# Turning attention probabilities with 16-bit DMA transposes instead of TensorE

## The chip, the cores and the metric

The kernel runs on one core of a Trainium2 chip. Its measure is the device time of one execution in microseconds. The five engines of a core are TensorE (PE in the rows, with PEld for its weight loads), VectorE (DVE), ScalarE (ACT), GpSimd (POOL) and SyncE (SP), whose queue issues most DMAs. Each engine runs its own list of instructions in order and waits on semaphores for the others. The DMA engines, 16 of them, move data beside all that.

## The reference, cut to what matters

A trunk of four layers works on 256 tokens of width 2048, in float32. Each layer normalises its input, multiplies it by one wide weight, splits the product into mixer inputs, memory queries and gates, runs a mixer (layers 0 and 3: a spatial gate; layer 1: forgetting attention; layer 2: differential attention) and a cross-attention to 256 memory tokens, gates both, and multiplies by an output weight. The part that the change touches is the second half of every attention, here that of the memory:

```python
logits = jnp.einsum('bshd,bmhd->bhsm', q, mem_k).astype(jnp.float32) * (HEAD_DIM ** -0.5)
p = jax.nn.softmax(logits, axis=-1).astype(mem_v.dtype)
return jnp.einsum('bhsm,bmhd->bshd', p, mem_v).reshape(B, S, MEM_WIDTH)
```

The probabilities `p` come out with the query along the partitions. TensorE needs the key there to multiply by the values, so every 128x128 block of `p` has to be turned. Differential attention turns the difference of two softmaxes.

The memory tokens are normalised too, `mem_n = rms_norm(mem, mem_norm_g)`. The kernel multiplies the raw memory by the weights and applies each token's factor afterwards.

## The kernel before

**Slots.** All weights, about 310 MB, stream through once. They are cut into 592 pieces of 128x1024 float32, and the program is a sequence of 592 *slots*, one for each piece. In a slot TensorE runs 12 matmuls of 128x512 (`slot_product`, lines 186 to 188): the weight and the activations are each split into a high and a low part, and three of the four products are taken. Eight slots make a *product* of 512 columns.

**What stands in one slot.** `between_slots` writes the rest of a slot in this order: `tick()` advances every running task (a Python generator) by one step; `split_until` splits the weight piece four slots ahead into its parts (ScalarE's cast at line 119, VectorE's subtraction at line 120); `load_until` issues the load of the piece eight slots ahead on SP (line 106); `run_late` writes what the tasks put off. There are four buffers for raw pieces and four for split ones. Engine lists are in the order written, so what a task writes in a slot stands ahead of that slot's cast, subtraction, load and matmuls.

**Attention.** `attention_task` (line 587) handles eight *units*, a unit being one head of one block of 128 queries. Step n writes, in order: the finishing of unit n-1 (a reciprocal; for differential attention the difference of the two softmaxes), the product of unit n-3 with the values (`av`, line 606), the turning of unit n-2 (`nc.tensor.transpose`, line 615, into a PSUM tile, and ScalarE's copy `pt` of it at line 619), the scores of unit n (lines 514, 531, 556), and the eviction of unit n-3's result by VectorE (line 629, or 627). A step takes one slot, for differential attention two for the first eight. There are 10 attentions: one of the memory in each layer and three in each of layers 1 and 2. A unit of the memory has two blocks to turn; in the other attentions the first four units have one and the last four two.

**The DMA transpose already in the kernel.** Other tensors are turned by `turn` and `join` (lines 360 to 375): ScalarE copies a 128x512 float32 tile, seen as 16-bit halves, into a plane of high halves and one of low halves (line 362); one `dma_start_transpose` on SP turns both planes (line 367); VectorE puts the halves together again (line 372).

**The start.** The first 16 slots make two products in turn, from the memory. The result of the first is scaled by the memory tokens' factors `r_mem` into `mvv` (ScalarE, line 404). `token_rms` computes these: over some slots it loads the memory's rows in four steps of two 256 KB tiles (SP, line 310), squares and sums them on ScalarE (line 303), and puts off the finish (VectorE lines 294 and 290, then a power on GpSimd, line 291). It is spawned with `delayed(3, ...)`, so that its first step falls into the third slot on.

**The end of layer 2.** The last differential attention ends near the end of the last gate product. `gate_task` multiplies its result with the gate (line 662), turns it with `turn` and `join`, and splits it into the parts `bh` and `bl` (lines 678 and 684) that the output product reads; these parts are needed in that product's seventh and eighth slots.

Of the kernel before, what the change touches and what calls it, by code (L numbers as in the profile page):

```python
# [9 lines left out]
F32 = mybir.dt.float32  # L10
F32R = mybir.dt.float32r
U16 = mybir.dt.uint16
# [8 lines left out]
P = 128  # L21
# [22 lines left out]
def trunk_kernel(  # L44
# [372 lines left out]
        yield from gen  # L417

    spawn(load_transposed(mem_t, "b", 4 * KT, bparts, early, 1, 2))
    spawn(delayed(3, token_rms(mem, r_mem)))  # L420
    first_accs = pair_product(lambda kp: bparts[kp])
    for i in range(DEPTH):
        acc = first_accs[0] if i == 0 else chunk_product(lambda kp: bparts[kp])
# [88 lines left out]
    def mem_scores(qt, mk, h, t):  # L512
        s = ps_s.tile([P, CW], F32, tag="s", name="s")
        nc.tensor.matmul(  # L514
            s[:, :S], qt[:, h, t * P : (t + 1) * P], mk[:, h * S : (h + 1) * S],
            start=True, stop=True,
        )
        st = small.tile([P, 8], F32, tag="sc", name="st")
        nc.vector.tensor_reduce(st[:, 0:1], s[:, :S], AX.X, ALU.max, negate=True)  # L519
        p = tmp.tile([P, S], F32, tag="p", name="p", bufs=4)  # L520
        late.append(
            lambda: nc.scalar.activation(
                p, s[:, :S], AF.Exp, bias=st[:, 0:1], accum_out=st[:, 1:2]
            )
        )
        return p, st, lambda: nc.vector.reciprocal(st[:, 2:3], st[:, 1:2])

    def fox_scores(qt, kt, h, hh, t, bias, cq):
# [10 lines left out]
        )  # L539
        st = small.tile([P, 8], F32, tag="sc", name="st")  # L540
        nc.vector.tensor_reduce(st[:, 0:1], lg[:, :w], AX.X, ALU.max, negate=True)
        p = tmp.tile([P, S], F32, tag="p", name="p", bufs=4)
        late.append(
            lambda: nc.scalar.activation(
                p[:, :w], lg[:, :w], AF.Exp, bias=st[:, 0:1], accum_out=st[:, 1:2]
# [4 lines left out]
    def diff_scores(qt, kt, h, t, bias):  # L550
# [10 lines left out]
        for m in range(2):  # L561
# [3 lines left out]
                scalar=BIG, op0=ALU.add, op1=ALU.min, accum_out=st[:, m : m + 1],  # L565
            )
            lgs.append(lg)
        ps = [tmp.tile([P, S], F32, tag="p", name="p", bufs=4) for m in range(2)]

        def exps():  # L570
            for m in range(2):
# [16 lines left out]
    def attention_task(scores, vv, finish, ready, diff=False, tiles=lambda t: t + 1):  # L588
# [2 lines left out]
        units = [(t, h) for t in range(2) for h in range(4)]  # L591
        mo = [tmp.tile([P, CW], F32, tag="mo", name="mo", bufs=6) for t in range(2)]
        made, turned = {}, {}
        for n in range(len(units) + 3):
            if 0 <= n - 1 < len(units):
                made[n - 1][2]()
            tb = None
            if 0 <= n - 3 < len(units) or 0 <= n - 2 < len(units):
                tb = ps_t.tile([P, CW], F32, tag="t", name="tb")
            if 0 <= n - 3 < len(units):  # L600
                t, h = units[n - 3]
                pt, done_st = turned.pop(n - 3)
                f = slice(h * HD, (h + 1) * HD)
                av = tb[:, 2 * P : 2 * P + HD]
                for j in range(tiles(t)):
                    nc.tensor.matmul(  # L606
                        av, pt[:, j * P : (j + 1) * P], vv[:, j, f],
                        start=(j == 0), stop=(j == tiles(t) - 1),
                    )
            if 0 <= n - 2 < len(units):  # L610
                t, h = units[n - 2]
                p, st, _ = made.pop(n - 2)
                nk = tiles(t)
                for j in range(nk):
                    nc.tensor.transpose(  # L615
                        tb[:, j * P : (j + 1) * P], p[:, j * P : (j + 1) * P], ident
                    )
                pt = tmp.tile([P, S], F32, tag="pt", name="pt")
                nc.scalar.copy(pt[:, : nk * P], tb[:, : nk * P])  # L619
                turned[n - 2] = (pt, st)  # L620
            if n < len(units):
                made[n] = scores(*units[n])
            if 0 <= n - 3 < len(units):
                t, h = units[n - 3]
                f = slice(h * HD, (h + 1) * HD)
                if diff:
                    nc.vector.tensor_copy(mo[t][:, f], av)
                else:
                    nc.vector.tensor_scalar(mo[t][:, f], av, done_st[:, 2:3], None, ALU.mult)
# [474 lines left out]
```

## Time and profile before

| | |
|---|---|
| median of 3 runs | 1737.36 us (1737.34 to 1737.95) |
| the profiled execution | 1737.19 us |
| its span, first to last instruction | 1735.4 us |
| TensorE busy | 1726.9 us |
| VectorE busy | 1076.3 us |
| ScalarE busy | 985.9 us |
| DMA queue of SP and ACT, share of 16 engines | 69.5% |

The span is what lies between the first and the last instruction; 1.8 us of the execution's time lie around it. The clock granted to TensorE was 1.000 of full speed as the mean of the whole span. Matmuls are pipelined: an instruction's own duration in the profile is longer than the distance to the next one's start, and the ends are modelled. The distance of starts is what an instruction takes from the stream.

### The profile page before, as it was taken

Reading aid. Unit: us, or ns where it says so; the run is one execution under the profiler, and the core shown is the slowest. Engines: PE = TensorE matmul, PEld = TensorE weight load, DVE = VectorE, ACT = ScalarE, POOL = GpSimd, SP = SyncE. Lnnn points to the kernel's source line nnn. Section 1 sums busy time; section 2 is a strip of 40 time slices with the busy share of each in tenths; the row PEclk is TensorE's granted clock in tenths of the full one; section 3 lists DMA queues with packets and bytes.
Section 4 is the critical chain, followed back from the end, with each engine's and each line's share of the span. In section 5 each row is a group of like instructions: output and inputs, shape, how many; then the busy total and the mean of one; then the engine's idle time right before and its main releaser. Section 6 shows DMA issues by size and latency. Waiting matters only on the chain.

```text
span 1735.4 us, 21890 instructions
## 1 busy us (share of the span) xinstructions
PE 1726.9 (100%) x7918; PEld 1423.2 (82%) x7918; DVE 1076.3 (62%) x1539; ACT 985.9 (57%) x1349; POOL 129.0 (7%) x156
## 2 busy tenths in 40 slices
PE   9999999999999999999999999999999999999999
PEld 6788888888888888888888887878788888888887
DVE  5547558555666656666666666767676656755553
ACT  5646645555655656555655565565665554565442
POOL 1110001000001101000000110302000000100000
PEclk9999999999999999999999999999999999999999
DMA  8888967567898676676788866766668876656674
GB/s 290 265 251 257 299 228 216 181 196 204 247 261 233 193 202 188 190 210 193 206 249 261 230 193 198 192 182 192 188 189 251 269 237 230 186 178 195 205 238 163
DMA packets 206957, 379.07 MB, mean 218 GB/s; under 512 B 113996, under 2 KB 116356, under 8 KB 206848
## 3 DMA queue, kind: packets, MB, share of 16 engines
q1 hardware_dynamic: 199584, 358.02, 69.5%
q0 software_dynamic: 5824, 18.44, 3.2%
q8 instruction: 62, 1.02, 0.2%
q10 hardware_dynamic: 1440, 1.21, 0.2%
q14 instruction: 47, 0.39, 0.1%
HBM read 339.55 MB, written 12.89 MB: 203 GB/s over the span
## 4 chain that ended last, share of the span: by engine, by line
PE 97%; DMA 2%; ACT 1%; DVE 0%; SPq 0%; issue 0%; POOL 0%; DVEq 0%; ACTq 0%
PE acc L186 31%; PE acc L187 30%; PE acc L188 30%; PE tb L606 2%; DMA xraw<-in_mem_t_dram 1%; PE tb L615 1%; PE s L514 1%; PE s L556 1%; DMA raw<-in_w_kv_dram 1%; PE sv L738 1%; PE s L531 0%; ACT whi L119 0%; DVE wlo L120 0%; PE acc L158 0%; ACT row L303 0%
## 5 line engine op out<-in xcount | busy, mean ns | idle before, releaser
L120 DVE TENSOR_TENSOR wlo<-raw,whi 128x1024 fp32r<-128x1024 f32 x591 | 720.1, 1223 | 476.6 <-ACT whi L119 471.9
L119 ACT CAST whi<-raw 128x1024 fp32r<-128x1024 f32 x591 | 617.6, 1050 | 466.1 <-PE acc L188 355.2
L186 PE MATMUL acc<-whi,xh 128*128 128x512 f32 x1600 | 637.3, 398 | 0.0
L188 PE MATMUL acc<-whi,xl 128*128 128x512 f32 x1600 | 623.9, 390 | 0.0
L187 PE MATMUL acc<-wlo,xh 128*128 128x512 f32 x1600 | 623.7, 390 | 0.0
L186 PEld LDWEIGHTS acc<-whi,xh 128*128 128x128 f32 x1600 | 300.6, 188 | 67.6 <-issue 4.2
L188 PEld LDWEIGHTS acc<-whi,xl 128*128 128x128 f32 x1600 | 300.3, 188 | 63.6
L187 PEld LDWEIGHTS acc<-wlo,xh 128*128 128x128 f32 x1600 | 300.7, 188 | 59.5
L186 PE MATMUL acc<-whi,bh 128*128 128x512 f32 x764 | 298.0, 390 | 2.2 <-ACT mvv L404 1.7
L187 PE MATMUL acc<-wlo,bh 128*128 128x512 f32 x764 | 297.9, 390 | 1.2 <-DVE wlo L120 1.2
L188 PE MATMUL acc<-whi,bl 128*128 128x512 f32 x764 | 297.4, 389 | 0.0
L186 PEld LDWEIGHTS acc<-whi,bh 128*128 128x128 f32 x764 | 143.5, 188 | 34.1 <-ACT mvv L404 2.1
L187 PEld LDWEIGHTS acc<-wlo,bh 128*128 128x128 f32 x764 | 143.5, 188 | 32.0 <-DVE wlo L120 2.0
L188 PEld LDWEIGHTS acc<-whi,bl 128*128 128x128 f32 x764 | 143.5, 188 | 29.9 <-DVE bl L222 0.4
L619 ACT COPY pt<-tb 128x256 f32<-128x256 f32 (+1 forms) x80 | 27.3, 341 | 124.1 <-PE tb L615 124.1
L338 POOL TENSOR_TENSOR sc<-sc,expo 128x8 f32<-128x8 f32 (+1 forms) x23 | 58.0, 2520 | 426.6 <-DVE sc L337 299.7
L362 ACT COPY pl<-sq 128x1024 uint16<-128x1024 uint16 x40 | 39.8, 1043 | 4.9 <-DVE sq L352 4.7
L221 ACT ACTIVATE xh<-wide,gk 128x256 fp32r<-128x256 f32 x48 | 20.5, 498 | 30.5 <-DVE wide L372 30.5
L372 DVE COPY wide<-xq 128x1024 uint16<-128x1024 uint16 x24 | 18.1, 754 | 29.5 <-DMA xq<-pl 29.1
L362 ACT COPY pl<-mo 128x1024 uint16<-128x1024 uint16 x32 | 31.9, 1044 | 7.6 <-DVE mo L662 7.6
L852 POOL DMA_DIRECT2D x_d<-xo x24 | 13.1, 547 | 292.9 <-DVE xo L851 292.1
L519 DVE TENSOR_REDUCE st<-s 128x1 f32<-128x256 f32 x32 | 13.5, 422 | 31.3 <-PE s L514 31.3
(170 smaller groups left out, 1002.6 us busy)
## 6 DMA issues: line engine op xcount, KB each, us to landing
raw<-in_w_a_dram SPq DMA_DIRECT2D x176, 512.0 KB, 4.2
raw<-in_w_o_dram SPq DMA_DIRECT2D x128, 512.0 KB, 4.4
raw<-in_w_b_dram SPq DMA_DIRECT2D x112, 512.0 KB, 4.1
raw<-in_w_c_dram SPq DMA_DIRECT2D x112, 512.0 KB, 4.0
raw<-in_w_kv_dram SPq DMA_DIRECT2D x63, 512.0 KB, 4.9
x_d<-xo POOLq DMA_DIRECT2D x24, 256.0 KB, 6.6
xo<-x_d SPq DMA_DIRECT2D x24, 256.0 KB, 5.9
lnp<-in_ln_dram SPq DMA_DIRECT2D x12, 256.0 KB, 5.9
```

The source lines that it names most:

```text
L119: nc.scalar.copy(hi, raw)
L120: nc.vector.tensor_sub(lo, raw, hi.bitcast(F32))
L186: nc.tensor.matmul(acc[t], xh[:, c], wh, start=begin, stop=False)
L187: nc.tensor.matmul(acc[t], xh[:, c], wl, start=False, stop=False)
L188: nc.tensor.matmul(acc[t], xl[:, c], wh, start=False, stop=end)
L221: nc.scalar.activation(hi, src, AF.Copy, scale=g)
L338: nc.gpsimd.tensor_tensor(sc[:, :, :n], sc[:, :, :n], expo.rearrange("p (a b) -> p a b", a=2)[:, :, :n], ALU.pow,)
L362: nc.scalar.copy(pl.rearrange("p (h e) -> p h e", h=2), src.bitcast(U16).rearrange("p (e h) -> p h e", h=2),)
L372: nc.vector.tensor_copy(wide[:, :, t, :].bitcast(U16).rearrange("p c (r h) -> p h c r", h=2), tts[t].rearrange("p (h c) r -> p h c r", h=2),)
L514: nc.tensor.matmul(s[:, :S], qt[:, h, t * P : (t + 1) * P], mk[:, h * S : (h + 1) * S], start=True, stop=True,)
L606: nc.tensor.matmul(av, pt[:, j * P : (j + 1) * P], vv[:, j, f], start=(j == 0), stop=(j == tiles(t) - 1),)
L619: nc.scalar.copy(pt[:, : nk * P], tb[:, : nk * P])
```

## The change

There are two edits.

The turning of a unit's probabilities leaves TensorE. Step n now copies unit n-2's probabilities into two planes of 16-bit halves (ScalarE, line 616 of the changed kernel), and SP issues one DMA transpose of both planes (line 621), back into the tile of the probabilities. `lag` steps later (two, for differential attention one) VectorE joins the halves into `pt` (line 629). The product with the values follows one step after that. The pipeline of eight units is so longer by `lag` and one step, and the probabilities have five buffers instead of four.

The memory rows' task is spawned with `delayed(2, ...)` instead of `delayed(3, ...)`.

```diff
-    spawn(delayed(3, token_rms(mem, r_mem)))
+    spawn(delayed(2, token_rms(mem, r_mem)))
...
-        p = tmp.tile([P, S], F32, tag="p", name="p", bufs=4)
+        p = tmp.tile([P, S], F32, tag="p", name="p", bufs=5)
...
-        for n in range(len(units) + 3):
+        lag = 1 if diff else 2
+        there = {}
+        for n in range(len(units) + 4 + lag):
...
-            if 0 <= n - 3 < len(units):
-                t, h = units[n - 3]
-                pt, done_st = turned.pop(n - 3)
-                f = slice(h * HD, (h + 1) * HD)
-                av = tb[:, 2 * P : 2 * P + HD]
+                av = tb[:, :HD]
...
-                for j in range(nk):
-                    nc.tensor.transpose(
-                        tb[:, j * P : (j + 1) * P], p[:, j * P : (j + 1) * P], ident
-                    )
-                pt = tmp.tile([P, S], F32, tag="pt", name="pt")
-                nc.scalar.copy(pt[:, : nk * P], tb[:, : nk * P])
-                turned[n - 2] = (pt, st)
+                w = tiles(t) * P
+                pl = tmp.tile([P, 2 * S], U16, tag="ppl", name="ppl", bufs=3)
+                nc.scalar.copy(
+                    pl[:, : 2 * w].rearrange("p (h e) -> p h e", h=2),
+                    p[:, :w].bitcast(U16).rearrange("p (e h) -> p h e", h=2),
+                )
+                tt = p[:, :w].bitcast(U16).rearrange("p (c r) -> p c r", r=P)
+                nc.sync.dma_start_transpose(tt, pl[:, : 2 * w])
+                there[n - 2] = (tt, st)
...
+            if 0 <= n - 2 - lag < len(units):
+                t, h = units[n - 2 - lag]
+                tt, st = there.pop(n - 2 - lag)
+                pt = tmp.tile([P, S], F32, tag="pt", name="pt")
+                nc.vector.tensor_copy(
+                    pt[:, : tiles(t) * P].bitcast(U16).rearrange("p (j r h) -> p h j r", h=2, r=P),
+                    tt.rearrange("p (h j) r -> p h j r", h=2),
+                )
+                turned[n - 2 - lag] = (pt, st)
```

On TensorE, in the memory attention of layer 0, between two slots' matmuls, the list before has the product with the values (`mv,pt`), the two transposes (`ident,p`) and the scores (`mk,mqt`):

```order
L187 MATMUL acc_2489<-wlo,xh_1207 128x512
L188 MATMUL acc_2489<-whi,xl_1208 128x512
L606 MATMUL tb<-mv,pt 128x128 x2
L615 MATMUL tb<-ident,p 128x128 x2
L514 MATMUL s<-mk,mqt 128x256
L186 MATMUL acc_2488<-whi,xh_1240 128x512
```

and in the changed kernel, at the same place:

```order
L187 MATMUL acc_2489<-wlo,xh_1207 128x512
L188 MATMUL acc_2489<-whi,xl_1208 128x512
L607 MATMUL tb<-mv,pt 128x128 x2
L514 MATMUL s<-mk,mqt 128x256
L186 MATMUL acc_2488<-whi,xh_1240 128x512
```

Only the transposes are gone; the product with the values now belongs to a unit two steps older.

On VectorE, in the same attention, two slots of the list before (a reciprocal, the scores' maximum, the eviction, the weight's subtraction `wlo`):

```order
L526 RECIPROCAL st<-st 128x1
L519 TENSOR_REDUCE st<-s 128x1
L629 TENSOR_SCALAR mo<-tb,st 128x128
L120 TENSOR_TENSOR wlo<-raw,whi 128x1024
L526 RECIPROCAL st<-st 128x1
L519 TENSOR_REDUCE st<-s 128x1
L629 TENSOR_SCALAR mo<-tb,st 128x128
L120 TENSOR_TENSOR wlo<-raw,whi 128x1024
```

and two slots in the changed kernel:

```order
L526 RECIPROCAL st<-st 128x1
L519 TENSOR_REDUCE st<-s 128x1
L629 COPY pt<-p 128x2x256
L640 TENSOR_SCALAR mo<-tb,st 128x128
L120 TENSOR_TENSOR wlo<-raw,whi 128x1024
L526 RECIPROCAL st<-st 128x1
L519 TENSOR_REDUCE st<-s 128x1
L629 COPY pt<-p 128x2x256
L640 TENSOR_SCALAR mo<-tb,st 128x128
L120 TENSOR_TENSOR wlo<-raw,whi 128x1024
```

The joining copy, which waits for the DMA transpose, stands between the scores' maximum and the eviction, ahead of the weight's subtraction.

On ScalarE at the start, the end of the list before ahead of the scaling of the first product (`bh` is the last memory part, `row` the memory norms' squares, `whi` the weight casts):

```order
L221 ACTIVATE bh_454<-xraw,gk 128x256 x2
L119 CAST whi<-raw 128x1024
L303 ACTIVATE row,ss<-row 128x512 x2
L119 CAST whi<-raw 128x1024 x3
L404 ACTIVATE mvv<-acc_169,r_mem 128x512
L404 ACTIVATE mvv<-acc_170,r_mem 128x512
```

and in the changed kernel:

```order
L221 ACTIVATE bh_454<-xraw,gk 128x256 x2
L303 ACTIVATE row,ss<-row 128x512 x2
L119 CAST whi<-raw 128x1024 x4
L404 ACTIVATE mvv<-acc_169,r_mem 128x512
L404 ACTIVATE mvv<-acc_170,r_mem 128x512
```

The last squares move ahead of one cast, not by a whole slot's work.

## Rows read from the trace of the kernel before

**Rows 1.** The first part: busy us (share of the span) xinstructions

```profile
PE 1726.9 (100%) x7918; PEld 1423.2 (82%) x7918; DVE 1076.3 (62%) x1539; ACT 985.9 (57%) x1349; POOL 129.0 (7%) x156
```

**Rows 2.** Groups by shape: xcount, busy us, mean ns, idle before

```profile
L615 PE MATMUL tb<-ident,p 128*128 128x128 f32 x136 | 27.9, 272 | 0.0
...
L619 ACT COPY pt<-tb 128x256 f32<-128x256 f32 x56 | 20.9, 373 | 88.9 <-PE tb L615 88.9
...
L619 ACT COPY pt<-tb 128x128 f32<-128x128 f32 x24 | 6.4, 266 | 35.2 <-PE tb L615 35.2
```

**Rows 3.** Timeline of TensorE, memory attention of layer 0: start us, us, instructions

```profile
312.41 0.60 PE L606 MATMUL tb<-mv,pt 128*128 128x128 f32 x4
...
316.28 0.60 PE L606 MATMUL tb<-mv,pt 128*128 128x128 f32 x4
316.72 0.38 PE L615 MATMUL tb<-ident,p 128*128 128x128 f32 x2
316.94 0.60 PE L514 MATMUL s<-mk,mqt 128*128 128x256 f32 x2
```

**Rows 4.** Timeline of VectorE, the same stretch

```profile
310.76 1.23 DVE L120 TENSOR_TENSOR wlo<-raw,whi 128x1024 fp32r<-128x1024 f32 x1 [0.23 <-ACT whi L119]
...
313.71 0.42 DVE L519 TENSOR_REDUCE st<-s 128x1 f32<-128x256 f32 x1 [1.65 <-PE s L514]
...
321.44 0.42 DVE L519 TENSOR_REDUCE st<-s 128x1 f32<-128x256 f32 x1 [1.59 <-PE s L514]
```

**Rows 5.** Timeline of ScalarE, the same stretch

```profile
310.63 0.48 ACT L522 ACTIVATE p<-s,st 128x256 f32<-128x256 f32 x1
...
313.33 0.37 ACT L619 COPY pt<-tb 128x256 f32<-128x256 f32 x1 [2.13 <-PE tb L615]
```

**Rows 6.** All DMA transposes: issue time on SP, ns, and landing

```profile
L367 SPq DMA_TRANSPOSE sq<-pl x40: 1242/1362/3721, 67.5 to 1490.7; - x40
...
DMA to landing us min/median/max: 2.9/5.4/8.2
```

**Rows 7.** Groups by shape: the plane split and the joining copy

```profile
L362 ACT COPY pl<-sq 128x1024 uint16<-128x1024 uint16 x40 | 39.8, 1043 | 4.9 <-DVE sq L352 4.7
...
L372 DVE COPY wide<-mo 128x1024 uint16<-128x1024 uint16 x32 | 23.4, 753 | 8.9 <-DMA mo<-pl 8.6
```

**Rows 8.** Windows: busy us of each engine, clock, DMA share, GB/s

```profile
300.00:333.00 33.00, 33.00 (x173) 28.18 (x172) 18.54 (x40) 18.38 (x37) 0.62 (x1) 1.00 0.49 158
333.00:340.00 7.00, 7.00 (x35) 5.84 (x34) 3.29 (x4) 4.41 (x5) 0.53 (x1) 1.00 0.93 253
```

**Rows 9.** Timeline of TensorE at the first products' end

```profile
52.65 0.39 PE L188 MATMUL acc<-whi,bl 128*128 128x512 f32 x1
54.74 0.50 PE L186 MATMUL acc<-whi,bh 128*128 128x512 f32 x1 [1.70 <-ACT mvv L404]
```

**Rows 10.** Timeline of ScalarE there

```profile
47.49 1.04 ACT L119 CAST whi<-raw 128x1024 fp32r<-128x1024 f32 x1
...
49.67 2.93 ACT L119 CAST whi<-raw 128x1024 fp32r<-128x1024 f32 x3
54.00 1.27 ACT L404 ACTIVATE mvv<-acc,r_mem 128x512 f32<-128x512 f32 x2 [1.40 <-POOL r_mem L291]
```

**Rows 11.** Timeline of VectorE there

```profile
51.88 0.15 DVE L294 TENSOR_REDUCE r_mem<-ss 128x2 f32<-128x8 f32 x1
```

**Rows 12.** Timeline of GpSimd there

```profile
52.32 1.64 POOL L291 TENSOR_TENSOR r_mem<-r_mem,expo 128x2 f32<-128x2 f32 x1 [46.85 <-DVE r_mem L290]
```

**Rows 13.** Timeline of VectorE at the end of layer 2's attention

```profile
1300.20 1.29 DVE L352 TENSOR_TENSOR mo<-mo,sc 128x512 f32<-128x512 f32 x2
...
1306.17 1.29 DVE L662 TENSOR_TENSOR mo<-mo,sg 128x512 f32<-128x512 f32 x2
...
1317.15 1.41 DVE L684 SCALAR_TENSOR_TENSOR bl<-wide,subg,bh 128x512 fp32r<-128x512 f32 x2
```

**Rows 14.** Timeline of TensorE where it reads that tile

```profile
1319.94 0.39 PE L188 MATMUL acc<-whi,bl 128*128 128x512 f32 x1
```

More of the change, by code (lines that the diff above doesn't have):

```diff
@@ L541, in fox_scores @@
         nc.vector.tensor_reduce(st[:, 0:1], lg[:, :w], AX.X, ALU.max, negate=True)
-        p = tmp.tile([P, S], F32, tag="p", name="p", bufs=4)
+        p = tmp.tile([P, S], F32, tag="p", name="p", bufs=5)
         late.append(
@@ L567, in diff_scores @@
             lgs.append(lg)
-        ps = [tmp.tile([P, S], F32, tag="p", name="p", bufs=4) for m in range(2)]
+        ps = [tmp.tile([P, S], F32, tag="p", name="p", bufs=5) for m in range(2)]
         def exps():
@@ L597, in attention_task @@
             tb = None
-            if 0 <= n - 3 < len(units) or 0 <= n - 2 < len(units):
+            if 0 <= n - 3 - lag < len(units):
+                t, h = units[n - 3 - lag]
+                pt, done_st = turned.pop(n - 3 - lag)
+                f = slice(h * HD, (h + 1) * HD)
                 tb = ps_t.tile([P, CW], F32, tag="t", name="tb")
-            if 0 <= n - 3 < len(units):
-                t, h = units[n - 3]
-                pt, done_st = turned.pop(n - 3)
-                f = slice(h * HD, (h + 1) * HD)
-                av = tb[:, 2 * P : 2 * P + HD]
+                av = tb[:, :HD]
                 for j in range(tiles(t)):
@@ L612, in attention_task @@
                 p, st, _ = made.pop(n - 2)
-                nk = tiles(t)
-                for j in range(nk):
-                    nc.tensor.transpose(
-                        tb[:, j * P : (j + 1) * P], p[:, j * P : (j + 1) * P], ident
-                    )
-                pt = tmp.tile([P, S], F32, tag="pt", name="pt")
-                nc.scalar.copy(pt[:, : nk * P], tb[:, : nk * P])
-                turned[n - 2] = (pt, st)
+                w = tiles(t) * P
[7 more added lines that the diff above has]
+                there[n - 2] = (tt, st)
             if n < len(units):
                 made[n] = scores(*units[n])
-            if 0 <= n - 3 < len(units):
-                t, h = units[n - 3]
+            if 0 <= n - 2 - lag < len(units):
[7 more added lines that the diff above has]
+                turned[n - 2 - lag] = (pt, st)
+            if 0 <= n - 3 - lag < len(units):
+                t, h = units[n - 3 - lag]
                 f = slice(h * HD, (h + 1) * HD)
```

## The prediction

> **What bounds the kernel now.** I read the first part of the page, then who waits for whom, then the groups of the changed lines by shape, and last the timeline of one attention slot and of the start. TensorE is busy for 1726.9 us of a span of 1735.4 us [rows 1]: it is the bound in every stage, and only 8.5 us are left outside it. So a microsecond that leaves TensorE's stream shortens the kernel by one, unless TensorE then waits; and a microsecond added to another engine costs nothing until TensorE waits for it. VectorE (62%) and ScalarE (57%) have room as means [rows 1]; what they do in an attention slot has to be looked at by itself.
>
> **Edit 1, what it removes.** There are 136 transposes on TensorE, with a mean duration of 272 ns [rows 2]. That is not their price: matmuls overlap, and what one takes is the distance from its start to the next one's. In the slot shown, two transposes start at 316.72 us and the scores behind them at 316.94 us, so one takes 0.11 us [rows 3]. The change takes nothing else off TensorE and puts nothing on it: the product with the values and the scores stay. 136 x 0.11 = 15.0 us leave the stream. ScalarE also loses 56 + 24 = 80 copies out of PSUM, 20.9 + 6.4 = 27.3 us, and its waits for TensorE ahead of them [rows 2]; that alone gives nothing.
>
> **What it adds, and what hides it.** Each of the 80 units (56 of 256 keys, 24 of 128 [rows 2]) gets three new instructions.
> ScalarE's plane split: 1024 halves take 1043 ns [rows 7], so about 0.52 us for 512 and 0.26 us for 256, in all 56 x 0.52 + 24 x 0.26 = 35 us, against the 27.3 us that go. It no longer waits for TensorE, since it reads what ScalarE or VectorE wrote a step before.
> VectorE's joining copy: 753 ns for 1024 [rows 7], so 0.38 or 0.19 us, in all 26 us. In the memory attention two slots start 316.28 - 312.41 = 3.87 us apart [rows 3], and VectorE was busy for 18.54 of 33 us, 56% [rows 8]; 0.38 us more on a slot of 3.65 us makes about 67%.
> The DMA transpose: SP is held for 1.36 us at the median by a transpose twice as large [rows 6], ahead of the slot's weight load. The weight load is written eight slots ahead, so a delay of this size lies inside its lead. For the DMA engines I price it from two windows. Without transposes, 158 GB/s took a share of 0.49, so a full share would be 322 GB/s. The window with two transposes of 262 KB moved 253 GB/s x 7 us = 1771 KB in 0.93 x 7 = 6.5 us; the other 1247 KB are 3.9 us at 322 GB/s, which leaves 1.3 us for one transpose [rows 8]. The new ones have half or a quarter of its bytes, 0.66 or 0.33 us: 45 us over the kernel, and a share of 0.49 + 0.66 / 3.65 = 0.67 in a slot of the memory attention. The queues stay below full there; for the time of one transpose they are near it, as the second window's 0.93 shows.
>
> **The new wait.** VectorE's joining copy waits for the DMA, and behind it in its list stand the eviction, the weight's subtraction and the next unit's reduction; TensorE's next product with the values waits for the copy. How much time is there? ScalarE's exponential of the slot starts at 310.63 us, lasts 0.48 us [rows 5] and is read out; with the split the planes are ready at about 311.8 us. SP comes free when the subtraction ends, at 310.76 + 1.23 = 312.0 us [rows 4]. So the transpose leaves at about 312.2 us. VectorE reaches the copy two slots on, behind the reduction at 321.44 + 0.42 us [rows 4], less 2 x 0.22 us for the shorter slots: 321.4 us. It has 9.2 us; the transposes of before land after 5.4 us at the median and 8.2 us at most [rows 6]. After the copy, 321.8 us, TensorE needs it only at its next visit, 316.28 + 2 x 3.87 - 3 x 0.22 = 323.4 us. In differential attention the lag is one step of two slots, which is the same distance. So I cost the wait at nothing. Its bounds: if it never binds, 0; with landings of 8.2 us plus the 1.3 us of another transpose ahead, 9.5 us, VectorE would stand for 0.3 us in a unit, still inside TensorE's 1.6 us. A gain from it is excluded, since TensorE has no wait in the attentions to lose.
>
> The Trainium skill ("VectorE: DVE Perf Modes", the three transpose paths and the rules for kernel authors) speaks against this edit: it gives 390 ns for a 128x128 block on TensorE and 1309 ns through the DMA crossbar, and advises TensorE where a PSUM destination will do. By its TensorE price 136 blocks would be 53 us and the time 1683 us, which shares the chance of rival C below; the trace's 0.11 us between starts does not agree with that price for a stream in flight, and the advice compares the two paths where nothing hides the slower one.
>
> **The end of layer 2.** There the longer pipeline is late: the last normalisation (two instructions, 1.29 us) stood at 1300.20 us and now comes directly ahead of the gate's multiplication at 1306.17 us [rows 13]. What hangs on it ends in `bl`, whose first half was done at 1317.15 + 0.75 = 1317.9 us, and TensorE reads it at 1319.94 us [rows 14]. A delay of 1.3 us leaves 0.7 us: no stall, with an upper bound of about 1 us if the chain grows.
>
> **Edit 2.** TensorE stood from 52.65 + 0.23 = 52.88 to 54.74 us, 1.86 us, for `mvv` [rows 9]; `mvv` waited for GpSimd's power of `r_mem`, that for VectorE's sum at 51.88 us [rows 10 to 12]. The order shows that ScalarE does the last squares one cast earlier, and VectorE the sum one subtraction earlier. Without the cast at 47.49 us (1.04 us, about 0.95 us of its stream) the squares end at about 48.7 instead of 49.67 us; then a cast and its subtraction, the sum at about 51.0 us. The power, 1.64 us [rows 12], ends at about 53.1 us and `mvv` starts there instead of at 54.00 us. The gain is 0.9 us. Bounds: nothing, if the rows land later among the first weight loads, and 1.86 us, if the stall goes whole.
>
> **The sum.** 1737.19 us (the profiled execution: 1735.4 us of span and 1.8 us around it) - 15.0 - 0.9 = 1721.3 us. The median of the runs lies 0.17 us above the profiled one, so I write 1721.5 us.
>
> **Rivals.**
> A. *The new way holds, but not everywhere.* In slots where norms, gates and attention meet on VectorE, the joining copy comes late and TensorE waits some tenths of a microsecond before the product with the values. For it: VectorE is in order, and a unit's copy can stand behind a norm's two instructions of 1.29 us, close to the 1.6 us of slack. Against it: such meetings are few. At 0.05 to 0.15 us as a mean of the 80 units it gives back 4 to 12 us: 1725 to 1733 us.
> B. *Slower: the landing outgrows the lag.* The place is the joining copy in the 56 units of lag two; the mechanism is that every landing exceeds 9.2 + 1.6 = 10.8 us, because transposes and weight loads crowd the 16 engines. Each microsecond above that stretches a slot by half of one. It decides from 15.9 / 56 x 2 = 0.6 us above, a landing of 11.4 us in every unit; at 12.5 us it costs 56 x 0.85 = 48 us, so 1769 us. Against it: a maximum of 8.2 us before [rows 6], and a share of 0.67.
> C. *TensorE's price is the duration, not the distance.* Then 136 x 0.272 = 37 us leave [rows 2], and the time is 1699 us. Against it: the starts 0.11 us apart [rows 3].
> D. *The early rows do nothing,* since the last squares follow the memory parts that ScalarE waits for anyway: 1722.4 us, inside my range.
>
> **How the numbers follow.** The forecast, with D, has 0.72, and by itself 1720 to 1724 us; A has 0.18, B 0.05, C 0.02, and 0.03 are left for a gain that other waits eat up to the old time. The range from 1719.5 to 1728 us holds the forecast and the nearer half of A: its lower end is 1737.36 - 15.0 - 1.9 with a microsecond for what I rounded, its upper end leaves out the rest of A, B and C. A change of under 0.2%, 3.5 us, can't be told from none. The forecast, A and C are faster by more than that, 0.92 together; B is slower, 0.05; the 0.03 lie within it.
>
> **What would show it.** In the changed profile line 615's group is gone, TensorE's busy time is about 15 us shorter and its idle time still near 8 us. TensorE's waits name neither line 629 nor a DMA; a row of that kind with several microseconds is rival A, and VectorE waiting for `p<-ppl` with landings over 10 us is rival B. At the start, TensorE's wait for `mvv` shrinks from 1.7 to about 0.8 us; unchanged, it is D. A late `bl` in layer 2's output product would show the step at its end wrong. The prediction is wrong if the time is above 1728 us, and its price for a transpose is wrong if it is below 1719 us.

## The result, and the profile after

The changed kernel takes 1723.76 us (median of 4 runs, 1723.05 to 1724.52), the kernel before 1737.37 us in the same series: a ratio of 0.9921, with a 95% interval from 0.9904 to 0.9938. It is faster by 13.6 us and inside the range; the forecast of 1721.5 us is 2.3 us too low. The profiled execution took 1723.05 us, which is 14.14 us less than that of before; the working below goes by these two. One run, of the kernel with two plane buffers below, took 2454.36 us at a granted clock of 0.654 and is left out of that kernel's time.

From the changed kernel's page: its span, the busy time of the engines, the queue that carries the weights and all DMA transposes, and the groups of the plane split and of the joining copy:

```profile
span 1721.2 us, 21817 instructions
...
PE 1712.4 (99%) x7782; PEld 1408.2 (82%) x7782; DVE 1096.8 (64%) x1619; ACT 1003.6 (58%) x1349; POOL 130.1 (8%) x156
...
q1 hardware_dynamic: 236960, 366.94, 74.3%
...
L616 ACT COPY ppl<-p 128x512 uint16<-128x512 uint16 (+1 forms) x80 | 43.7, 546 | 4.2 <-DVE p L581 4.2
L629 DVE COPY pt<-p 128x512 uint16<-128x512 uint16 (+1 forms) x80 | 33.0, 413 | 15.6 <-DMA p<-ppl 15.6
```

Against [rows 1] TensorE has 136 instructions and 14.5 us less; line 615's group of [rows 2] is gone. TensorE is idle for 8.8 us of the span, for 8.5 us before. The same queue on the page of before, in packets, MB and share of the 16 engines:

```profile
q1 hardware_dynamic: 199584, 358.02, 69.5%
```

Its packets took 0.743 x 1721.2 - 0.695 x 1735.4 = 73 us more of the 16 engines, for 8.9 MB more. Counted by packet size in the two traces, 31 us of these lie in the 256-byte packets of the DMA transposes (133,120 for 98,304), 11 us in packets of 4 bytes, and 30 us in the 4096-byte packets of the other loads, whose number is the same.

The waits of TensorE in the changed kernel (us in total, times, longest):

```profile
PE warm_ps L269 <- DVE warm L266: 1.2, 1, 1.2
PE acc L187 <- DVE wlo L120: 1.2, 2, 0.7
PE acc L186 <- ACT whi L273: 1.1, 2, 0.6
PE tb L607 <- DVE pt L629: 0.9, 2, 0.7
PE acc L187 <- DVE wlo L274: 0.5, 2, 0.2
```

The fourth row is the new wait, and it is small. The wait for `mvv` on line 404, of 1.7 us before [rows 9], is gone.

The memory attention of layer 0, on TensorE and then on VectorE, and its window (the columns of [rows 8]):

```profile
312.86 0.60 PE L607 MATMUL tb<-mv,pt 128*128 128x128 f32 x4
...
316.47 0.60 PE L607 MATMUL tb<-mv,pt 128*128 128x128 f32 x4
```

```profile
313.93 0.42 DVE L519 TENSOR_REDUCE st<-s 128x1 f32<-128x256 f32 x1 [1.65 <-PE s L514]
314.27 0.45 DVE L629 COPY pt<-p 128x512 uint16<-128x512 uint16 x1
```

```profile
300.00:333.00 33.00, 33.00 (x162) 27.91 (x162) 21.91 (x44) 23.08 (x38) 0.65 (x1) 1.00 0.82 201
```

A slot of the attention now takes 316.47 - 312.86 = 3.61 us, where it took 3.87 us [rows 3]. VectorE begins the joining copy right behind the scores' maximum, without a wait. The DMA share rose from 0.49 [rows 8] to 0.82; the 4096-byte packets in this window took 238 ns each, for 202 ns before.

All new DMA transposes, as [rows 6] shows the old ones (time on SP in ns; who waited, us and times; landing):

```profile
L621 SPq DMA_TRANSPOSE p<-ppl x80: 1167/1188/2018, 302.3 to 1522.2; - x80
...
  DVE pt L629: 15.6, 12
...
DMA to landing us min/median/max: 3.1/4.2/7.3
```

They land after 4.2 us at the median, and VectorE waited for 12 of the 80.

The start of the program, on ScalarE, VectorE and TensorE, where [rows 9 to 11] stood:

```profile
45.63 0.91 ACT L221 ACTIVATE bh<-xraw,gk 128x256 fp32r<-128x256 f32 x2 [1.02 <-DMA xraw<-in_mem_t_dram]
...
52.00 1.27 ACT L404 ACTIVATE mvv<-acc,r_mem 128x512 f32<-128x512 f32 x2 [0.31 <-POOL r_mem L291]
```

```profile
49.88 0.15 DVE L294 TENSOR_REDUCE r_mem<-ss 128x2 f32<-128x8 f32 x1
```

```profile
52.85 0.39 PE L188 MATMUL acc<-whi,bl 128*128 128x512 f32 x1
53.08 0.39 PE L186 MATMUL acc<-whi,bh 128*128 128x512 f32 x1
```

`r_mem`'s sum is done 2.0 us earlier and so is `mvv`; TensorE goes from one product to the next without a gap. It stood still for 1.86 us there before [rows 9].

Where the 14.2 us come from is read by the distance between the starts of the same matmul in the two traces. The changed kernel's lead grows by 1.79 us up to 184 us of its span (start and edit 2), by 1.86 us in each of the four memory attentions (7.44 us for 64 transposes), by 3.03 us in the three forgetting attentions and by 1.93 us in the three differential ones (36 transposes each): 14.19 us.

The differential attentions keep half of what their transposes cost. The place is the end of each of them in layer 2. Here is the end of the third, on SP, VectorE and TensorE:

```profile
1274.26 1.19 SPq L621 DMA_TRANSPOSE p<-ppl  x1
```

```profile
1270.85 0.46 DVE L629 COPY pt<-p 128x512 uint16<-128x512 uint16 x1
...
1274.25 0.47 DVE L629 COPY pt<-p 128x512 uint16<-128x512 uint16 x1 [0.44 <-DMA p<-ppl]
...
1278.86 0.46 DVE L629 COPY pt<-p 128x512 uint16<-128x512 uint16 x1 [2.55 <-DMA p<-ppl]
```

```profile
1268.67 0.39 PE L188 MATMUL acc<-whi,xl 128*128 128x512 f32 x1
1268.90 0.60 PE L607 MATMUL tb<-vv,pt 128*128 128x128 f32 x4
1269.26 0.48 PE L186 MATMUL acc<-whi,xh 128*128 128x512 f32 x1
1269.58 0.40 PE L187 MATMUL acc<-wlo,xh 128*128 128x512 f32 x1
...
1278.33 0.39 PE L188 MATMUL acc<-whi,xl 128*128 128x512 f32 x1
1279.37 0.71 PE L607 MATMUL tb<-vv,pt 128*128 128x128 f32 x4 [0.65 <-DVE pt L629]
```

The last unit's transpose leaves at 1274.26 us; VectorE stands before its joining copy for 2.55 us, and TensorE's product starts 1.04 us behind the matmul ahead of it, where the same pair at 1268.67 us is 0.23 us apart. Over the three attentions four products are late, by 0.19, 0.37, 0.18 and 0.81 us, and one elsewhere by 0.1 us: about 1.7 us. They don't have one cause. The products late by 0.37 and 0.81 us are those of a last unit (unit 7; units count from 0), whose copy waits for its transpose. The two of 0.19 and 0.18 us, in the first and the second attention, are those of unit 5. Its copy doesn't wait for the DMA; it stands in VectorE's list behind two reductions of a norm and the combination of unit 7's two score maps. This is the first of them:

```profile
1097.96 1.27 DVE L334 TENSOR_REDUCE sc<-sq 128x8 f32<-128x512 f32 x2
...
1100.59 0.45 DVE L629 COPY pt<-p 128x512 uint16<-128x512 uint16 x1
```

### The profile page after: what moved, and what is told of

The parts are those of the page before. It is cut to its first block, busy times and chain, and to the rows that moved or that the text cites. A ratio compares the mean times of both kernels' runs of the same rounds, so it can differ in the third digit from the quotient of the medians.

```text
span 1721.2 us, 21817 instructions
## 1 busy us (share of the span) xinstructions
PE 1712.4 (99%) x7782; PEld 1408.2 (82%) x7782; DVE 1096.8 (64%) x1619; ACT 1003.6 (58%) x1349; POOL 130.1 (8%) x156
## 4 chain that ended last, share of the span: by engine, by line
PE 96%; DMA 2%; DVE 1%; ACT 0%; issue 0%; SPq 0%; DVEq 0%; ACTq 0%
PE acc L186 31%; PE acc L187 30%; PE acc L188 30%; PE tb L607 2%; PE s L514 1%; DMA xraw<-in_mem_t_dram 1%; PE s L556 1%; DMA raw<-in_w_kv_dram 1%; PE sv L749 1%; DMA p<-ppl 1%; PE s L531 0%; DVE wlo L120 0%; ACT whi L119 0%; PE acc L158 0%; ACT row L303 0%
## 5 line engine op out<-in xcount | busy, mean ns | idle before, releaser
L362 ACT COPY pl<-sq 128x1024 uint16<-128x1024 uint16 x40 | 39.8, 1043 | 14.2 <-DVE sq L352 14.2
L616 ACT COPY ppl<-p 128x512 uint16<-128x512 uint16 (+1 forms) x80 | 43.7, 546 | 4.2 <-DVE p L581 4.2
L629 DVE COPY pt<-p 128x512 uint16<-128x512 uint16 (+1 forms) x80 | 33.0, 413 | 15.6 <-DMA p<-ppl 15.6
```

What stands on the lines that cost most here:

```text
L362: nc.scalar.copy(pl.rearrange("p (h e) -> p h e", h=2), src.bitcast(U16).rearrange("p (e h) -> p h e", h=2),)
L616: nc.scalar.copy(pl[:, : 2 * w].rearrange("p (h e) -> p h e", h=2), p[:, :w].bitcast(U16).rearrange("p (e h) -> p h e", h=2),)
L629: nc.vector.tensor_copy(pt[:, : tiles(t) * P].bitcast(U16).rearrange("p (j r h) -> p h j r", h=2, r=P), tt.rearrange("p (h j) r -> p h j r ...
```

## The experiments

Each ratio is to a series of the kernel before on the same chip: 1736.88 us for the doubled TensorE transposes, each edit alone and the first cure; 1737.38 us for the left-out DMA way, the second cure, half of the lag and the first version of twice the transposes; 1737.2 us for the other four.

**What a transpose costs TensorE.** Every transpose of the kernel before runs twice.

```diff
-                for j in range(nk):
+                for j in [j for j in range(nk) for _ in range(2)]:
                     nc.tensor.transpose(
```

> The kernel before with each of the 136 transposes on TensorE run twice, into the same place. Theory: a transpose costs the distance of starts, 0.11 us, so 15.0 us more: 1752.4 us. Rival C of the prediction: it costs its own duration of 272 ns, 37 us more: 1774 us. Third: TensorE's visits to attention have slack inside, and the second transposes cost less than 10 us.

Measured: 1752.45 us (1751.94 to 1753.27), ratio 1.0088 (1.0074 to 1.0102). That is 15.6 us for 136 transposes, 0.1145 us each; in the traces 15.0 us between the end of the start and the end of the kernel, 0.110 us each. TensorE in the memory attention:

```profile
313.62 0.60 PE L615 MATMUL tb<-ident,p 128*128 128x128 f32 x4
314.06 0.60 PE L514 MATMUL s<-mk,mqt 128*128 128x256 f32 x2
```

Four transposes take 0.44 us of the stream, while the page gives each of them 272 ns as before. The price is the distance between starts; rival C is out. The Trainium skill ("VectorE: DVE Perf Modes", the three transpose paths) gives 390 ns for a 128x128 bf16 block on TensorE. This run does not agree with that as a price in a stream: a float32 block cost 0.1145 us.

**What the DMA way costs.** The transposes on the DMA are left out, and the joining copy reads the planes, so the probabilities are not turned. The probabilities have four buffers here instead of five, the planes four instead of three.

```diff
...
-                tt = p[:, :w].bitcast(U16).rearrange("p (c r) -> p c r", r=P)
-                nc.sync.dma_start_transpose(tt, pl[:, : 2 * w])
+                tt = pl[:, : 2 * w].rearrange("p (c r) -> p c r", r=P)
```

> The changed kernel without the DMA transposes of the probabilities: VectorE joins the halves straight from the planes, so the probabilities aren't turned. All else stays. Theory: outside of TensorE's waits in layer 2's last steps (1.6 us) the DMA costs nothing, so the time is about 1722.1 us, with no wait of TensorE at line 607. Rival: the transposes also slow the weight loads or hold SP in ways that cost elsewhere; then the time falls further, below 1720 us.

Measured: 1721.78 us (1720.98 to 1722.34), ratio 0.991 (0.9895 to 0.9925). Without any DMA transpose of the probabilities the kernel gains some 2 us over the changed one: in the traces 1.4 us in the differential attentions, 0.5 us at the start, before the first new transpose, and 0.1 us elsewhere. So the 73 us of DMA time and the 80 x 1.19 us on SP cost no more than 1.5 us. The list of TensorE's waits has no line 607 here, but the products of unit 5 are as late as in the changed kernel, by 0.19 us each; the first of them:

```profile
1100.08 0.39 PE L188 MATMUL acc<-whi,xl 128*128 128x512 f32 x1
1100.50 0.71 PE L607 MATMUL tb<-vv,pt 128*128 128x128 f32 x4
```

Their lateness is VectorE's order, not the DMA's.

**Edit 2 alone.** The kernel before, with the memory rows' task one slot earlier:

```diff
-    spawn(delayed(3, token_rms(mem, r_mem)))
+    spawn(delayed(2, token_rms(mem, r_mem)))
```

> Edit 2 alone, on the kernel before. Theory: the whole wait of TensorE for mvv goes, 1.86 us at the first products' end, as the changed kernel's trace shows it gone, and the first slots lose nothing lasting: about 1735.6 us. First rival, the prediction's own term: the sum of r_mem comes one cast earlier and no more, 0.9 us: 1736.5 us. Second rival: the memory parts decide when the squares are done, and the gain belongs to the first loads' chance of the run: 1737.4 us, with TensorE still waiting about 1.7 us for mvv.

Measured: 1736.14 us (1734.78 to 1737.12), ratio 0.9994 (0.9985 to 1.0003): the runs alone can't tell it from none. The trace can; TensorE's waits are

```profile
PE acc L187 <- DVE wlo L120: 1.5, 2, 0.8
PE warm_ps L269 <- DVE warm L266: 1.2, 1, 1.2
```

and `mvv` isn't among them. From 184 us on its lead over the trace of before stays at 1.89 us.

**Edit 1 alone.** The changed kernel with `delayed(3, ...)`:

```diff
-    spawn(delayed(2, token_rms(mem, r_mem)))
+    spawn(delayed(3, token_rms(mem, r_mem)))
```

> Edit 1 alone: the changed kernel with the memory rows fetched from the third slot on again. Theory: the edits are independent, since one lies in the first 55 us and the other behind 290 us; edit 1 is worth 12.4 us in the profiled lead (7.4 in the four memory attentions, 3.0 in forgetting, 1.9 in differential attention), and the time is the changed kernel's plus 1.8 us, about 1725.5 us. Rival: the wait for mvv isn't what edit 2 took away, and the time stays at 1723.8 us.

Measured: 1725.09 us (1724.35 to 1726.17), ratio 0.993 (0.9916 to 0.9943). TensorE's first waits:

```profile
PE tb L607 <- DVE pt L629: 2.1, 2, 1.9
PE acc L186 <- ACT mvv L404: 1.7, 1, 1.7
```

Edit 1 brings most of the gain, 11.8 us in the runs. The stall for `mvv` is back.

**The tail of differential attention, first cure.** There a step is two slots while units are being made (n below 8) and one slot after that. So for units 6 and 7 the joining copy stands one slot behind the transpose, and not two. This version combines the two score maps in the second slot of the unit's own step and issues the transpose one step earlier, so every unit has two slots or more for it. It changes a second thing with it: no combination stands in the same slot ahead of a joining copy in VectorE's list any more.

```diff
-            if 0 <= n - 1 < len(units):
+            if not diff and 0 <= n - 1 < len(units):
                 made[n - 1][2]()
...
-            if 0 <= n - 2 < len(units):
-                t, h = units[n - 2]
-                p, st, _ = made.pop(n - 2)
+            u = n - 1 if diff else n - 2
+            if 0 <= u < len(units):
+                t, h = units[u]
+                p, st, _ = made.pop(u)
...
             if diff and n < len(units):
                 yield
+                made[n][2]()
```

> The changed kernel with differential attention's difference of the softmaxes taken in the second slot of its own step, and the plane split and DMA transpose one step earlier; the joining copy stays where it is. So the last two units, whose steps are one slot wide, have two slots between transpose and copy instead of one. Theory: TensorE's waits of 1.6 us ahead of line 607 in layer 2 come from that one-slot distance; they go, and the time is about 1722.2 us with less spread. Rival: VectorE's list is too full there for the copy to be in time (rival A of the prediction); the work on VectorE is the same, the waits stay and so does 1723.8 us.

Measured: 1721.14 us (1720.7 to 1721.38), ratio 0.9907 (0.9893 to 0.992). All of TensorE's waits, and then VectorE's last joining copies of the third differential attention:

```profile
PE acc L187 <- DVE wlo L120: 1.3, 2, 0.8
PE warm_ps L269 <- DVE warm L266: 1.2, 1, 1.2
```

```profile
1271.68 0.47 DVE L630 COPY pt<-p 128x512 uint16<-128x512 uint16 x1
...
1274.18 0.46 DVE L630 COPY pt<-p 128x512 uint16<-128x512 uint16 x1
```

In the differential attentions no copy waits and no product is late. Against the changed kernel's trace it gains 0.75, 0.27 and 0.90 us in the three of them. By the kernel without DMA transposes, which gains 1.39 us there, the way over the DMA, the one-slot step, is the cause of about 1.4 of these 1.9 us; the other 0.5 us are VectorE's order. Elsewhere VectorE still waits for five copies, 6.7 us, and in the first forgetting attention one product is 0.25 us late behind a copy that waited for 2.69 us; that attention gains 0.4 us less here than in the changed kernel's trace.

**The tail, second cure.** The two-slot step is kept for three steps more:

```diff
-            if diff and n < len(units):
+            if diff and n < len(units) + 3:
                 yield
```

> The changed kernel with two slots for three more steps of each differential attention, so that every joining copy has two slots, at the price that the attention ends three slots later. Theory: TensorE's waits at line 607 go (1.6 us), but layer 2's last attention now ends at the slot where its gate's result is due, and TensorE waits there for the gate's multiplication, its two transposes and the splits, 5 to 9 us once: 1727 to 1732 us. Rival: that chain still has room (the prediction saw 0.7 us left for a delay of 1.3 us), and the time is 1722 us.

Measured: 1728.72 us (1727.04 to 1729.04), ratio 0.9947 (0.993 to 0.9964): slower than the changed kernel. The wait on line 607 is gone, but TensorE has a new one:

```profile
PE acc L186 <- ACT bh L689: 3.4, 1, 3.4
```

The attention ends three slots later, the chain of normalisation, gate and layout behind it too, and the output product of layer 2 comes to a slot without its operand: 6.8 us are lost there. That is twice the wait. Behind it the granted clock is at the lower of its two levels, half of full speed, for 6.8 us, and the matmuls start 0.43 us apart instead of 0.23. The window (the columns of [rows 8]):

```profile
1309.50:1316.40 6.90, 6.33 (x15) 4.66 (x16) 2.19 (x3) 1.74 (x3) 0.00 (x0) 0.51 0.53 155
```

The room lies ahead of the transposes; behind them there is too little.

**Half of the lag.** A lag of one step everywhere:

```diff
-        lag = 1 if diff else 2
+        lag = 1
```

> The changed kernel with a lag of one step in all attentions, so that in memory and forgetting attention, too, only one slot of about 3.5 us lies between a transpose and the joining copy. Theory: the distance of two slots is what hides the way over the DMA; a transpose lands 4.2 us after its issue at the median, so with one slot VectorE waits in nearly each of the 56 units and TensorE, whose next product follows a slot later, waits some tenths to 1 us in many of them: 1730 to 1760 us, with TensorE's waits named line 607 behind line 629. Rival: VectorE's and TensorE's own slack covers it, and the time stays within 2 us of 1723.8 us.

Measured: 1744.6 us (1742.06 to 1746.39), ratio 1.004 (1.0026 to 1.0055): slower than before. TensorE's first wait, and VectorE's for the new transposes:

```profile
PE tb L607 <- DVE pt L629: 12.8, 10, 4.8
```

```profile
DVE pt L629 <- DMA p<-ppl: 51.0, 29, 6.4
```

The landing is what it was (4.1 us at the median, 8.6 at most), a slot of 3.6 us is not enough for it, and 19 us go in the memory and forgetting attentions of layers 0 to 2. Of these some 3.4 us are the clock's: after two of TensorE's waits, of 4.8 and 2.0 us, it is granted half of full speed for 3.4 us each. This is rival B's mechanism with the lag halved instead of the landing grown: the second slot of the lag is worth more than the change.

**Twice the transposes.** The first cure, with every new transpose issued a second time into a spare tile, ahead of the real one (and two buffers of planes, for space):

```diff
-                pl = tmp.tile([P, 2 * S], U16, tag="ppl", name="ppl", bufs=3)
+                pl = tmp.tile([P, 2 * S], U16, tag="ppl", name="ppl", bufs=2)
...
+                spare = tmp.tile([P, S], F32, tag="spare", name="spare", bufs=1)
+                sp = spare[:, :w].bitcast(U16).rearrange("p (c r) -> p c r", r=P)
+                nc.sync.dma_start_transpose(sp, pl[:, : 2 * w])
```

> The kernel of e_early (difference taken in its own step) with each new DMA transpose issued twice, first into a spare tile; two plane buffers instead of three make room for that tile. Theory: queue and DMA engines have room in the attentions, a transpose's landing grows by one or two microseconds and stays inside the two slots: 1721 to 1722 us. Rival B of the prediction, in its mechanism: transposes crowd SP and the 16 engines near their limit, so a doubled number costs 5 us or more, as waits of TensorE at line 607 or of ScalarE for raw weights.

Measured: 1746.75 us (1739.18 to 1751.41), ratio 1.0049 (1.0035 to 1.0064). I had expected room for it, and there is none: TensorE waits for 16.3 us on its product with the values. But ScalarE now waits for planes to come free:

```profile
ACT ppl L617 <- DMA p<-ppl: 45.6, 17, 6.3
```

so buffers and traffic had to be told apart, by the next two.

**Two buffers alone.** The first cure with two buffers of planes and single transposes:

```diff
-                pl = tmp.tile([P, 2 * S], U16, tag="ppl", name="ppl", bufs=3)
+                pl = tmp.tile([P, 2 * S], U16, tag="ppl", name="ppl", bufs=2)
```

> e_early with two plane buffers instead of three and single transposes: the other half of e_dma2. If the two buffers caused its loss, ScalarE waits for the planes here, too, and the time is 1725 to 1745 us. If the loss needs the doubled transposes, the plane is free in time (a step of 3.2 us or more between splits, 4.2 us to landing, two buffers) and the time stays within 1 us of 1721.1 us.

Measured: 1721.5, 1721.63 and 1722.55 us, ratio 0.9909 (0.9891 to 0.9927). ScalarE waits for planes here, too, 18.0 us in 10 times, but the time doesn't show it: two buffers are enough for single transposes.

**Twice the transposes, three buffers.** The spare copies go into a tile that is free by then, in layers 1 to 3 alone (72 of 80 units):

```diff
+                if state["slot"] > 184:
+                    sp = lam_row[:, :w].bitcast(U16).rearrange("p (c r) -> p c r", r=P)
+                    nc.sync.dma_start_transpose(sp, pl[:, : 2 * w])
```

> The doubled DMA transposes again, without the confound of e_dma2: three plane buffers as in e_early; the first of each pair goes into a tile that is no longer used, so layer 0's memory attention (8 units) is left with single ones and 72 units are doubled. Theory now: most of e_dma2's loss came from its two plane buffers, since ScalarE waited 45.6 us there for a transpose to free a plane; with three, at most 3 us remain: 1721 to 1724 us. Rival B in its mechanism: SP and the DMA engines are near their limit with twice the transposes; 1735 us or more, with ScalarE not waiting for planes but TensorE for line 629's copy.

Measured: 1742.2 us (1739.6 to 1749.62), ratio 1.0037 (1.0023 to 1.005). My expectation failed again. TensorE's first wait, SP's waits, and the landing of the real transposes:

```profile
PE tb L607 <- DVE pt L633: 12.9, 9, 3.3
```

```profile
SPq L624 <- DMA lam_row<-ppl: 37.7, 32, 4.3
```

```profile
L625 SPq DMA_TRANSPOSE p<-ppl x80: 1167/1257/2337, 302.1 to 1541.6; - x80
...
DMA to landing us min/median/max: 2.3/3.3/7.9
```

Once issued, the real transpose lands no later than before (3.3 us). It is issued later: SP is held for 1.2 us by each of the two, and waits up to 4.3 us for the last spare copy to land, since all go to one tile. The share of the DMA queues in the stretch from 570 to 618 us rose only from 0.88 to 0.91. The loss against the first cure is 17.9 us between the traces and 20.4 us between the medians of one series. Part of it is the clock: it is at half of full speed for 3.4 us of this trace, behind a wait of 3.3 us, and the mean clock of the ten runs was 0.995 to 0.999. How the rest is shared between SP, the DMA engines, which were already near full, and the wait that the single spare tile adds stays open.

**Both kernels again, side by side.** The changed kernel and the first cure, on one chip in one series, with no further edit:

> The changed kernel once more, beside e_early on the same chip: 1723.8 us, with waits of TensorE at line 607 in layer 2's last steps between 1 and 3 us, different in each run.

> e_early once more beside the changed kernel on the same chip. Theory: its gain of 1.6 us or more over the changed kernel repeats, 1721 to 1722 us. Rival: the difference between the two lay in the chips and their runs, and both medians come within 1 us.

Measured: 1724.88 us (1723.19 to 1726.13), ratio 0.9925 (0.9913 to 0.9937), and 1721.83 us (1720.83 to 1722.54), ratio 0.9907 (0.9894 to 0.9921). No run of the one lies in the range of the other. The first cure is the best version here, by 2 to 3 us. In this trace of the changed kernel TensorE waits for 2.1 us on line 607, and the three differential attentions gain 0.43 us together; with edit 1 alone they gain 0.70 us, in the first trace 1.93 us, and in both traces of the first cure 3.86 us. So the shortfall differs from execution to execution, by the traces from 2.0 to 3.5 us.

## Why the prediction was right, and where it was off

**The price of a transpose: right.** 136 x 0.11 us was the main term, and doubling the transposes measured 0.1145 us each. TensorE's busy time fell by 14.5 us.

**"So I cost the wait at nothing": right but for 0.1 us in two of the three kinds of attention.** In the memory attention of layer 0 the transpose left at 312.62 us for a forecast of 312.2, and VectorE reached its copy 8.9 us later for 9.2. Landings were shorter than those I used, 4.2 us at the median and 7.3 at most for 5.4 and 8.2, so the slack was larger than I said.

**"In differential attention the lag is one step of two slots, which is the same distance": wrong.** This is the step that failed. The code shows it: the second `yield` of a step is made only while `n < len(units)`. The last two units have one slot, about 3.2 us, for a landing of 4.2 us. It cost 1.4 us in this trace (the differential attentions gain 1.93 us here and 3.32 us without the DMA transposes). A second thing was priced at nothing with it: in this pipeline the copy of unit 5 stands directly behind the combination of unit 7, and where a norm's reductions come ahead of both, its product is late; that cost 0.5 us (3.32 us against 3.86 us of the first cure).

**Edit 2: the removed cast right, the whole gain half its size.** I gave it 0.9 us for the removed cast; the traces show 1.8 to 1.9 us, the whole stall, as in the upper bound. The cast's part holds: from ScalarE's start on the last memory part to `r_mem`'s sum it is 5.2 us in each of the three traces without edit 2 and 4.25 us in each of the eleven with it, 0.95 us less. The other microsecond came from that memory part itself, which ScalarE started at 45.63 us, 1.0 us earlier than in the trace of before. It waits there for a DMA [the first row of the start above], and I had held that arrival fixed. It is no fixed gain: the part is started at 46.7 to 47.1 us without edit 2 and at 45.4 to 47.3 us with it, and TensorE's lead at 200 us is 0.44 to 2.28 us over the eleven traces, for -0.3 us in the two other kernels without edit 2. The wait for `mvv` is gone in all eleven. Between runs the start differs by as much as the edit gives: with edit 2 alone the median moved by 0.7 us.

**A term that I left out.** In the forgetting attentions 36 transposes gave 3.03 us instead of 3.96. The longer pipeline makes TensorE interrupt its stream in more slots: in the third of them in 13 instead of 11. The rows at 1269.26 us show what hangs on that: behind a visit the first matmul starts its successor after 0.32 us instead of 0.23. In the trace of that attention these first matmuls lose 0.19 us, the other matmuls of the visited slots, each a few ns slower, another 0.24, and the visits themselves are 0.16 us shorter than by their transposes alone: 1.32 + 0.16 - 0.19 - 0.24 = 1.05 us. The kernel without DMA transposes gains the same 1.05 us there, so it is the pipeline's doing and not the transfers'. But the number of visits alone does not explain it. The memory attention of layer 0 goes from 11 to 13 visited slots, too, and gains 1.86 us for 1.76 us of transposes: there the first matmuls lose 0.15 us, and the others of the visited slots gain 0.08 us instead of losing. What makes those others slower in one attention and not in the other stays open; no run changed the visits by themselves.

**The end of layer 2: right.** The normalisation stands directly ahead of the gate, and `bl` ([rows 13] before) comes at 1305.87 us:

```profile
1293.84 1.29 DVE L352 TENSOR_TENSOR mo<-mo,sc 128x512 f32<-128x512 f32 x2
1295.04 1.29 DVE L673 TENSOR_TENSOR mo<-mo,sg 128x512 f32<-128x512 f32 x2
...
1305.87 1.41 DVE L695 SCALAR_TENSOR_TENSOR bl<-wide,subg,bh 128x512 fp32r<-128x512 f32 x2
```

TensorE's lead there is 12.33 us, so `bl` is 1305.87 + 12.33 - 1317.15 = 1.05 us late against TensorE, for a forecast of 1.3 us, and TensorE doesn't wait. Its first half, by the prediction's 0.75 us, was done at 1306.6 us and read at 1307.6 us. The second cure shows that this room ends: its chain comes some 7 us later still, and TensorE stood for 3.4 us.

**The costs beside the path: too low, without effect.** The plane splits took 43.7 us for a forecast of 35, the joining copies 33.0 for 26: half the columns cost more than half the time. The DMA queue took 73 us more for a forecast of 45, a share of 0.82 in the memory attention for 0.67. The transposes' own packets make up 31 us of this, or 42 us with those of 4 bytes, close to the price; the forecast left out that the other loads' packets would take longer beside them. "The queues stay below full there" held, with less to spare.

**The sum.** Forecast for the profiled execution: a gain of 15.9 us; measured 14.1. The differences are -1.4 (the short step), -0.6 (the rest of the differential attentions, VectorE's order above all), -0.9 (the forgetting attentions), +0.9 (edit 2) and +0.4 (the memory attentions). They partly cancel, and that is luck: without the earlier arrival of the memory part the total would be 0.9 us further off. In the second series the median was 1724.88 us, inside the range but above the 1720 to 1724 us that the forecast gave itself.

**The rivals.** A came true in mechanism and not in size: five late products, 1.7 us in all where it asked for 4 to 12, and mostly because of the short step; two of them, of 0.19 and 0.18 us, stood behind a norm's reductions as A had it. B did not happen, the longest landing being 7.3 us against 11.4; but half the lag or twice the transposes, 17 to 23 us slower than the changed kernel, show that it was not far away. C fell with the doubled transposes, D with `mvv`'s wait.

## What to carry to other kernels

Where TensorE is the bound, a transpose that TensorE does costs the distance between starts, and a way round it that is many times slower (here a landing after 4.2 us for two blocks of 0.11 us) is still nearly free if the code gives it room in time: here two slots, where one was not enough. Count that room at the ends of a pipeline too, in slots as the code makes them there, since its steps may be shorter once nothing new goes in. Take the room ahead of the consumer and not by ending later, where what follows has its own due time, as the end of layer 2 had. And count a stall of TensorE for more than its length: in the second cure the lower clock behind it cost as much again.

## What the runs showed of the hardware that was not expected

- DMA transposes slow the loads beside them: in the window from 300 to 333 us the 4096-byte packets of the weight loads took 238 ns each in the changed kernel, 202 ns before and 202 ns in the kernel without the new transposes. The transposes' own packets, of 256 bytes, took 0.4 us of all 16 engines for each of the 80 (31 us), and 11 us more went to packets of 4 bytes.
- SP is held for nearly as long by a small transpose as by a large one: at least 1.17 us by the new ones of 131 and 66 KB, at least 1.23 us by those of 262 KB in the same trace. Nor does the landing follow the size: 4.2 us at the median for the new ones, and 4.1, 5.2 and 6.5 us for the three kinds of 262 KB (`mo`, `sq`, `xq`).
- The clock doubled the price of a stall. In the second cure TensorE stood for 3.4 us and was then granted half of full speed for 6.8 us, which cost another 3.4 us. In the five cases of this kind behind the start (second cure, half of the lag, twice the transposes) it had just stood for 2.0 to 4.8 us; others in the same traces, of up to 3.3 us, had no such stretch behind them.
- A stream of matmuls can pay for a visit to other work behind it: the first matmul starts its successor after 0.32 us (in the memory attention up to 0.42 us) instead of 0.23, and the rest of the slot is 0.01 to 0.06 us slower, by what the visit was.
- Issuing the DMA transposes twice made the kernel 20 us slower than its base, although TensorE, VectorE and ScalarE did the same work.
